# A hybrid decoder layer: the Mamba branch in a written-out TensorE order, with one z projection moved

## The chip, the cores and the metric

The kernel runs on one core of a Trainium2 chip. Its engines are TensorE (PE in the profile, with PEld for its weight loads), VectorE (DVE), ScalarE (ACT), GpSimd (POOL) and SyncE (SP, which here only issues DMAs). The metric is the device time of one execution in microseconds (us); several runs are summed up by their median.

## What is computed

One decoder layer on x (512 tokens of 1024 features, float32). A combined projection feeds an attention branch, a Mamba-2 branch and two gates; both branches are projected back, merged and projected, and then follow a layer norm, a SwiGLU feed-forward block and a second layer norm. The change lies in the Mamba branch, which has four groups of eight heads:

```python
def mamba2_branch(z, xbc, dt_raw, conv_w, conv_b, dt_bias, a_log, d_skip, norm_w):
    xbc = silu(causal_depthwise_conv(xbc, conv_w, conv_b))
    xs, bm, cm = split(xbc)
    dt = softplus(dt_raw + dt_bias)
    a = -exp(a_log)
    y = ssd_chunked(xs, dt, a, bm, cm) + d_skip[:, None] * xs
    u = (y * silu(z)).reshape(bsz, seq, SSM_GROUPS, -1)
    u = u * rsqrt(mean(square(u), -1) + RMS_EPS)
    return u * norm_w
# ssd_chunked, for each chunk of 128 tokens:
#   decay = exp(acum_l - acum_s) below the diagonal, acum = cumsum(dt * a)
#   y_diag = (C B^T * decay) (x dt);  state of the chunk = B^T (x dt decay_to_end)
#   h = h_prev * chunk_decay + state;  y_off = exp(acum) * C h_prev
```

## The kernel before

Every wide product is made of three matmuls (`mm3`, L144 to L147), since each operand is split into a high part and a low part (`split`, L102: ScalarE writes the high part, VectorE the rest). A **step** below is one such `mm3` with 512 columns. Weights come in chunks of 512 KB on SP's queue into four `raw` slots (`fetch_w`); three slots each hold the split halves. PSUM has four banks for wide accumulations (`gps`) and four for everything else (`cps`).

For each group g the Mamba branch does this:

- `group_bc` projects B and C (two blocks of 8 steps). `conv_evac` applies the convolution of four taps (ScalarE, three VectorE operations at L282) and a tanh, `silu_to` one more VectorE operation. Then B is transposed to token order (L306) and C·B of each chunk is formed and masked (L312, L313).
- `group_x` projects half of x (16 steps, two blocks), evacuates each in the same way and transposes it into `xtok` (L328, L329). It is called twice a group.
- `group_z` projects z (four banks, 32 steps) and writes tanh-gated values into the only `gz` slot (L337, L338).
- `group_y` runs over the four chunks: xdt on VectorE (L355); for each half of the heads a decay block loaded by SP from DRAM (`ac_d`, L361), five ScalarE operations on it (L364, L365), and a product with C·B on VectorE (L366); the y products (L370); dx on POOL (L373); the sum (L376); the product with the state of the chunks before (L379) and its two VectorE operations (L381, L382); xw on POOL (L385), the new state (L387) and its update (L392, L393).
- `group_u` multiplies y by the gate (L403), squares and sums it (ScalarE, L405), takes the power -1/2 on POOL (L407), scales (L408), transposes (L412) and splits.
- `group_proj` multiplies u by a quarter of the projection (32 steps) and adds the result to `sd` (ScalarE for group 0, VectorE at L424 otherwise).

Which instruction comes when: a scheduler at build time plays the program through with its own costs, and gives each engine the ready instruction of the best priority. Priorities follow the text of the program; inside `high_priority` they are raised. Inside `manual_schedule(engines=...)` the named engines keep the order of the text. On the chip each engine then executes its list strictly in that order. In the kernel before, the first z projection has TensorE, ScalarE and VectorE in text order; ScalarE stays so until `entry.close()`, which stands behind the softplus of dt and the exponential of a_log. The Mamba branch behind it (L588 to about L690) leaves TensorE to the scheduler, and the attention stage that follows has TensorE in text order again:

```python
    for g in range(NG):
        ys = group_y(g, st)
        if g == 0:
            st = group_bc(1)
            group_x(1, st, 0)
        else:
            group_proj(g - 1, u)
            gz = group_z(g)
        u = group_u(g, ys, gz)
```

Of the kernel before, what the change touches and what calls it, by code (L numbers as in the profile page):

```python
# [18 lines left out]
P = 128  # L19
# [23 lines left out]
def tile_hybrid_decoder_layer(  # L43
# [247 lines left out]
    def group_bc(g):  # L291
        st = {}
# [5 lines left out]
        for bi, nm in ((0, "bT"), (1, "cT")):  # L298
            v, th = conv_evac(16 + 4 * bi + g, gp[bi])
            st[nm] = slot(nm)  # L300
            silu_to(st[nm], v, th)
        bT, cT = st["bT"], st["cT"]
        btok = st["btok"] = slot("btok")
        ps = cps()
        for c in range(NT):
            nc.tensor.transpose(out=ps[:, c * P:(c + 1) * P], in_=bT[:, c * P:(c + 1) * P], identity=ident)  # L306
        nc.scalar.copy(out=btok, in_=ps)
        cbm = st["cbm"] = slot("cbm", (P, NT, P))
        ps = cps()
        for c in range(NT):  # L310
            cs = slice(c * P, (c + 1) * P)
            nc.tensor.matmul(out=ps[:, cs], lhsT=bT[:, cs], rhs=cT[:, cs], start=True, stop=True)  # L312
        nc.vector.tensor_tensor(out=cbm, in0=ps.rearrange("p (c l) -> p c l", c=NT),  # L313
                                in1=tri.rearrange("p (o l) -> p o l", o=1).broadcast_to([P, NT, P]), op=ALU.mult)
        st["xtok"] = big("xtok")
        return st

    def group_x(g, st, pair):
        xtok = st["xtok"]

        def evac(b, ps):
            j = 2 * pair + b
            v, th = conv_evac(4 * g + j, ps)
            xst = slot("xst")
            silu_to(xst, v, th)
            pt = cps()
            for c in range(NT):
                nc.tensor.transpose(out=pt[:, c * P:(c + 1) * P], in_=xst[:, c * P:(c + 1) * P], identity=ident)  # L328
            nc.scalar.copy(out=xtok[:, :, j * P:(j + 1) * P], in_=pt.rearrange("p (c f) -> p c f", c=NT))  # L329
        gemm_ws(w_in, C_X + g * 512 + pair * 256, KD, rhs_x, evac)  # L330
# [820 lines left out]
```

## Time and profile before

| | |
|---|---|
| median of 3 runs | 1131.83 us (1131.39 to 1133.82) |
| the profiled execution | 1133.8 us, span 1132.1 us |
| TensorE busy | 1104.3 us (98% of the span), 6086 matmuls |
| VectorE busy | 777.6 us (69%) |
| ScalarE busy | 526.7 us (47%) |
| GpSimd busy | 134.4 us (12%) |
| DMA | 134.20 MB, mean 119 GB/s |

The span is what the profile sees of one execution; the time of the run lies a little above it. Busy time of TensorE counts each matmul with a modelled end, and dense matmuls overlap, so the start times of neighbouring matmuls say more about lost time than the busy share does.

### The profile page before, as it was taken

The numbers are of one execution on the slowest core, as the hardware profiler recorded it, in microseconds if no ns is written. First come the engines' busy times: TensorE is split into PE (matmuls) and PEld (weight loads), VectorE is DVE, ScalarE is ACT, GpSimd is POOL, SyncE is SP. The second block draws the span as 40 slices with busy tenths as digits, with TensorE's granted clock in tenths as the row PEclk, the third lists the DMA queues.
The fourth block names the chain that finished last, engine by engine and source line by source line (L and its number), as shares of the span: only waits on it lengthen the run. The fifth ranks groups of instructions, "written<-read, shape, count | busy, mean of one in ns | idle before, by whom it ended". The sixth has DMA issues, their size and how long they took to land.

```text
span 1132.1 us, 15815 instructions
## 1 busy us (share of the span) xinstructions
PE 1104.3 (98%) x6086; PEld 942.8 (83%) x6086; DVE 777.6 (69%) x1223; ACT 526.7 (47%) x912; POOL 134.4 (12%) x165
## 2 busy tenths in 40 slices
PE   7999999999999999999999999999999999999996
PEld 5887778777787878888888888888999999988885
DVE  2679973885688473788778744556997777777326
ACT  2477764454442341567566544313654555453210
POOL 3003130020114000122110000011111111100001
PEclk9999999999999999999999999999999999999999
DMA  6353243243231333321222135381788787565212
GB/s 198 111 169 108 84 128 93 75 124 100 75 94 59 94 91 93 91 61 57 75 75 75 57 114 184 101 214 42 210 197 208 184 204 159 103 233 176 93 56 75
DMA packets 116059, 134.20 MB, mean 119 GB/s; under 512 B 5668, under 2 KB 94480, under 8 KB 115856
## 3 DMA queue, kind: packets, MB, share of 16 engines
q1 hardware_dynamic: 98896, 111.75, 32.3%
q0 software_dynamic: 14640, 14.10, 7.6%
q10 hardware_dynamic: 2448, 7.34, 1.9%
q8 instruction: 48, 0.79, 0.3%
q14 instruction: 27, 0.22, 0.1%
HBM read 128.78 MB, written 4.26 MB: 118 GB/s over the span
## 4 chain that ended last, share of the span: by engine, by line
PE 80%; DVE 9%; issue 4%; DMA 3%; POOL 2%; ACT 2%; POOLq 0%; DVEq 0%; ACTq 0%
PE gps L147 19%; PE gps L146 19%; PE gps L145 19%; PE cps L146 5%; PE cps L147 5%; PE cps L145 4%; PE cps L509 2%; DVE wlo L104 2%; PE cps L370 1%; PE cps L499 1%; ACT whi L103 1%; DMA rq<-in_w_ffn_up_dram 1%; PE cps L474 1%; PE cps L475 1%; PE cps L328 1%
## 5 line engine op out<-in xcount | busy, mean ns | idle before, releaser
L104 DVE TENSOR_TENSOR wlo<-raw,whi 128x1024 fp32r<-128x1024 f32 x127 | 156.2, 1230 | 176.4 <-ACT whi L103 175.1
L103 ACT CAST whi<-raw 128x1024 fp32r<-128x1024 f32 x127 | 133.5, 1051 | 244.3 <-PE gps L146 97.8
L145 PE MATMUL gps<-xh,whi 128*128 128x512 f32 x456 | 180.9, 397 | 0.0
L147 PE MATMUL gps<-xh,wlo 128*128 128x512 f32 x456 | 179.6, 394 | 0.0
L146 PE MATMUL gps<-xl,whi 128*128 128x512 f32 x456 | 179.3, 393 | 0.0
L103 ACT CAST wh<-rq 128x1024 fp32r<-128x1024 f32 (+1 forms) x84 | 82.1, 979 | 94.5 <-PE cps L146 42.7
L104 DVE TENSOR_TENSOR wl<-rq,wh 128x1024 fp32r<-128x1024 f32 (+1 forms) x84 | 94.8, 1132 | 29.5 <-ACT wh L103 29.3
L147 PEld LDWEIGHTS gps<-xh,wlo 128*128 128x128 f32 x456 | 86.1, 189 | 17.5
L145 PEld LDWEIGHTS gps<-xh,whi 128*128 128x128 f32 x456 | 86.0, 189 | 17.3 <-issue 0.2
L146 PEld LDWEIGHTS gps<-xl,whi 128*128 128x128 f32 x456 | 86.0, 189 | 17.3 <-issue 0.2
L145 PE MATMUL gps<-whi,xh 128*128 128x512 f32 x192 | 76.3, 398 | 1.9 <-ACT whi L103 1.6
L146 PE MATMUL gps<-wlo,xh 128*128 128x512 f32 x192 | 75.6, 394 | 1.2 <-DVE wlo L104 1.2
L147 PE MATMUL gps<-whi,xl 128*128 128x512 f32 x192 | 75.5, 393 | 0.0
L282 DVE SCALAR_TENSOR_TENSOR t_v<-gps,cw,t_v 128x511 f32<-128x511 f32 (+2 forms) x72 | 53.4, 744 | 3.8 <-ACT t_v L279 3.1
L146 PE MATMUL gps<-t_ul,whi 128*128 128x512 f32 x128 | 51.1, 399 | 0.0
L147 PE MATMUL gps<-t_uh,wlo 128*128 128x512 f32 x128 | 51.0, 399 | 0.0
L145 PE MATMUL gps<-t_uh,whi 128*128 128x512 f32 x128 | 50.5, 395 | 0.0
L481 ACT ACTIVATE t_y<-t_y,sm 128x128 f32<-128x128 f32 (+1 forms) x64 | 35.6, 558 | 21.1 <-DVE sm L479 21.0
L145 PEld LDWEIGHTS gps<-whi,xh 128*128 128x128 f32 x192 | 36.4, 190 | 10.5 <-ACT whi L103 2.3
L146 PEld LDWEIGHTS gps<-wlo,xh 128*128 128x128 f32 x192 | 36.4, 190 | 9.4 <-DVE wlo L104 2.0
L364 ACT ACTIVATE t_ab<-t_ab,acum 128x128 f32<-128x128 f32 x128 | 41.6, 391 | 4.7 <-DMA t_ab<-ac_d 2.7
L147 PEld LDWEIGHTS gps<-whi,xl 128*128 128x128 f32 x192 | 36.3, 189 | 8.5 <-DVE xl L104 1.1
(567 smaller groups left out, 2717.0 us busy)
## 6 DMA issues: line engine op xcount, KB each, us to landing
raw<-in_w_in_dram SPq DMA_DIRECT2D x80, 512.0 KB, 3.7
rq<-in_w_ffn_gate_dram SPq DMA_DIRECT2D x25, 512.0 KB, 5.9
rq<-in_w_ffn_up_dram SPq DMA_DIRECT2D x25, 512.0 KB, 6.3
raw<-in_w_ffn_down_dram SPq DMA_DIRECT2D x22, 512.0 KB, 3.8
t_ab<-ac_d SPq DMA_DIRECT2D x32, 256.0 KB, 3.2
raw<-in_w_proj_ssm_dram SPq DMA_DIRECT2D x16, 512.0 KB, 3.5
rq<-in_w_ffn_gate_dram POOLq DMA_DIRECT2D x10, 512.0 KB, 8.4
rq<-in_w_ffn_up_dram POOLq DMA_DIRECT2D x10, 512.0 KB, 6.2
```

The source lines that it names most:

```text
L103: nc.scalar.copy(out=hi, in_=src)
L104: nc.vector.tensor_tensor(out=lo, in0=src, in1=hi.bitcast(F32), op=ALU.subtract)
L145: nc.tensor.matmul(out=o, lhsT=l[0], rhs=r[0], start=start, stop=False, skip_group_check=skip)
L146: nc.tensor.matmul(out=o, lhsT=l[0], rhs=r[1], start=False, stop=False, skip_group_check=skip)
L147: nc.tensor.matmul(out=o, lhsT=l[1], rhs=r[0], start=False, stop=stop, skip_group_check=skip)
L282: nc.vector.scalar_tensor_tensor(out=v[:, sh:], in0=ps[:, 0:T - sh], scalar=cw[:, k, blk:blk + 1], in1=v[:, sh:], op0=ALU.mult, op1=ALU.add)
L328: nc.tensor.transpose(out=pt[:, c * P:(c + 1) * P], in_=xst[:, c * P:(c + 1) * P], identity=ident)
L364: nc.scalar.activation(out=m[:, r, :], in_=m[:, r, :], func=AF.Relu, scale=-1.0, bias=acum[:, c, h:h + 1])
L370: nc.tensor.matmul(out=py[:, r * 64:(r + 1) * 64], lhsT=ms[r // 4][:, r % 4, :], rhs=xdt[:, r * 64:(r + 1) * 64], start=True, stop=True)
L474: nc.tensor.matmul(out=ps[:, 0:n], lhsT=q1[:, qs], rhs=k1[:, 0:n], start=True, stop=False)
L481: nc.scalar.activation(out=pt[:, 0:n], in_=pt[:, 0:n], func=AF.Exp, scale=-1.0, bias=sm[:, 2:3], accum_out=sm[:, 0:1])
L509: nc.tensor.matmul(out=po[:, kb * P:], lhsT=vt[:, kb, hh, :], rhs=pT[kb][j], start=kb == 0 and j == 0, stop=kb == NT - 1 and j == 1)
```

## The change

The functions of the Mamba branch become generators that yield after every step. TensorE's order from the first B and C projection to the last Mamba projection is now the order of the text (`manual_schedule`), and the text deals out the steps: `run(steps, n)` takes n steps of the wide products, `pace(steps, ns, what)` alternates between them and the parts of `what` (the parameters, y or u), which it issues with raised priority. Small products that need an evacuation first (the transposes of B and of x, C·B) are put into `later` and issued 14 or 15 steps on. The evacuations of B, C and x get raised priority. In y, xw and dx are issued ahead of the y products, xw first, and the state's update ahead of the sums. In u, the norms of all four chunks come first and the transposes later, one chunk every three steps. The z projection of group 1 moves from behind the projection of group 0 to between the two halves of x of group 1; z of groups 2 and 3 stays where it was. `params` holds what stood behind the dt projection: softplus, cumulative sums and the transposes and DMA of the decay. Of its two exponentials, that of a_log stays in ScalarE's ordered part (now directly behind the copy of the dt projection), and that of the softplus leaves it.

```diff
-    def group_bc(g):
+
+    later = []
+
+    def run(steps, n=10 ** 6):
+        for _ in range(n):
+            if next(steps, 0) == 0:
+                return
+            for e in later:
+                e[0] -= 1
+            while later and later[0][0] <= 0:
+                later.pop(0)[1]()
+
+    def bc_steps(g, st):
         gp = [gps() for _ in range(2)]
+
+        def b_tok():
...
+            nc.scalar.copy(out=btok, in_=ps)
...
+        def c_b():
...
         for bi, c0 in ((0, C_B + g * P), (1, C_C + g * P)):
             hi, lo = load_w(w_in[:, c0:c0 + P], 8, P)
             for kt in range(KD):
                 mm3(gp[bi], (hi[kt], lo[kt]), rhs_x(kt), kt == 0, kt == KD - 1)
+                if kt == KD - 1:
+                    nm = ("bT", "cT")[bi]
+                    with tc.high_priority():
+                        v, th = conv_evac(16 + 4 * bi + g, gp[bi])
+                        st[nm] = slot(nm)
+                        silu_to(st[nm], v, th)
+                    later.append([14, (b_tok, c_b)[bi]])
+                yield 1
...
+    def x_steps(g, st, pair):
+        if pair == 0:
+            st["xtok"] = big("xtok")
         xtok = st["xtok"]
...
+            with tc.high_priority():
+                v, th = conv_evac(4 * g + j, ps)
+                xst = slot("xst")
+                silu_to(xst, v, th)
+
+            def to_tokens():
...
+                with tc.high_priority():
+                    nc.scalar.copy(out=xtok[:, :, j * P:(j + 1) * P], in_=pt.rearrange("p (c f) -> p c f", c=NT))
+            later.append([15, to_tokens])
+        yield from ws_steps(w_in, C_X + g * 512 + pair * 256, KD, rhs_x, evac)
...
+        if before is None:
+            return gz, xs_steps(w_in, C_Z + g * 512, lhs_x, evac)
...
-    def group_y(g, st):
+    def y_steps(g, st, ys):
...
+            if c < NT - 1:
+                xw = slot("xw")
+                nc.gpsimd.tensor_tensor(out=v8(xw), in0=v8(xc), in1=bc8(dtw, c), op=ALU.mult)
+            dx = slot("dx")
+            nc.gpsimd.tensor_tensor(out=v8(dx), in0=v8(xc),
+                                    in1=d_bc[:, h8].rearrange("p (h o) -> p h o", o=1).broadcast_to([P, 8, 64]), op=ALU.mult)
+            yield 1
             py = cps()
             for r in range(8):
                 nc.tensor.matmul(out=py[:, r * 64:(r + 1) * 64], lhsT=ms[r // 4][:, r % 4, :], rhs=xdt[:, r * 64:(r + 1) * 64],
                                  start=True, stop=True)
-            dx = slot("dx")
-            nc.gpsimd.tensor_tensor(out=v8(dx), in0=v8(xc),
-                                    in1=d_bc[:, h8].rearrange("p (h o) -> p h o", o=1).broadcast_to([P, 8, 64]), op=ALU.mult)
-            y = slot("y")
...
             if c > 0:
                 po = cps()
...
-                yo = slot("yo")
-                nc.vector.tensor_tensor(out=v8(yo), in0=v8(po), in1=bc8(ecum, c), op=ALU.mult)
-                nc.vector.tensor_tensor(out=y, in0=y, in1=yo, op=ALU.add)
             if c < NT - 1:
-                xw = slot("xw")
-                nc.gpsimd.tensor_tensor(out=v8(xw), in0=v8(xc), in1=bc8(dtw, c), op=ALU.mult)
...
+            y = slot("y")
+            nc.vector.tensor_tensor(out=y, in0=py, in1=dx, op=ALU.add)
+            if c > 0:
+                yo = slot("yo")
+                nc.vector.tensor_tensor(out=v8(yo), in0=v8(po), in1=bc8(ecum, c), op=ALU.mult)
+                nc.vector.tensor_tensor(out=y, in0=y, in1=yo, op=ALU.add)
             ys.append(y)
-        return ys
-
-    def group_u(g, ys, gz):
+            yield 1
...
+    def u_steps(g, ys, gz):
...
+        yield 1
...
             pu = cps()
...
             split(uh[:, :, cs], ul[:, :, cs], pu.rearrange("p (j t) -> p j t", j=4))
-        return uh, ul
-
-    def group_proj(g, u):
-        uh, ul = u
+            yield 1
...
     ea = carve(SH)
     nc.scalar.activation(out=ea, in_=a_bc, func=AF.Exp)
     entry.close()
-    da = carve(NT, SH)
...
+    def params():
+
+        ps = cps()
+        for tt in range(NT):
+            nc.tensor.transpose(out=ps[:, tt * 48:(tt + 1) * 48], in_=fdT[0:48, tt * P:(tt + 1) * P], identity=ident[0:48, 0:48])
...
+        yield 1
+        daf = da.rearrange("p t h -> p (t h)")
+        ps = cps()
+        nc.tensor.matmul(out=ps[:, 0:128], lhsT=tri, rhs=daf, start=True, stop=True)
+        nc.tensor.matmul(out=ps[:, 128:256], lhsT=ones, rhs=daf, start=True, stop=True)
...
+        yield 1
+        acT = carve(T)
+        ps = cps()
+        for tt in range(NT):
+            nc.tensor.transpose(out=ps[0:32, tt * P:(tt + 1) * P], in_=acum[:, tt, :], identity=ident)
+        nc.scalar.copy(out=acT[0:32], in_=ps[0:32])
+        nc.sync.dma_start(out=ac_d.rearrange("c h l -> h c l"), in_=acT[0:32].rearrange("h (c l) -> h c l", c=NT))
...
+        yield 1
...
-    st = group_bc(0)
-    for pair in range(2):
-        group_x(0, st, pair)
-    nw_bc = slot("nw", (P, 2048))
-    nc.sync.dma_start(out=nw_bc, in_=ssm_norm_w.partition_broadcast(P))
+    sts = [{} for _ in range(NG)]
     qk = {}
-    u = None
-    for g in range(NG):
-        ys = group_y(g, st)
-        if g == 0:
-            st = group_bc(1)
-            group_x(1, st, 0)
-        else:
-            group_proj(g - 1, u)
-            gz = group_z(g)
-        u = group_u(g, ys, gz)
-        if g == 0:
-            group_x(1, st, 1)
-        elif g < NG - 1:
-            st = group_bc(g + 1)
-            for pair in range(2):
-                group_x(g + 1, st, pair)
-    for isq in (True, False):
-        for _ in att_qk(0, isq, qk):
-            pass
-    group_proj(NG - 1, u)
+    u = [None]
+
+    def pace(steps, ns, what):
+
+        for n in ns:
+            run(steps, n)
+            with tc.high_priority():
+                next(what)
+
+    def bcx(g):
+        return chain(bc_steps(g, sts[g]), x_steps(g, sts[g], 0), x_steps(g, sts[g], 1))
+
+    def z_steps(g):
+        gz[0], steps = group_z(g)
+        yield from steps
+
+    gz = [gz]
+    with tc.manual_schedule(engines={mybir.EngineType.PE}):
+        after = bcx(0)
+        pace(after, (3, 20, 5), params())
+        nw_bc = slot("nw", (P, 2048))
+        nc.sync.dma_start(out=nw_bc, in_=ssm_norm_w.partition_broadcast(P))
+        run(after)
+        for g in range(NG):
+            after = bcx(g + 1) if g < NG - 1 else chain(att_qk(0, True, qk), att_qk(0, False, qk))
+            ys = []
+            if g == 0:
+                after = chain(bc_steps(1, sts[1]), x_steps(1, sts[1], 0), z_steps(1), x_steps(1, sts[1], 1))
+                run(after, 16)
+                pace(after, (0, 2, 0, 5, 0, 5, 0, 4), y_steps(g, sts[g], ys))
+                pace(after, (0, 9, 3, 3, 3), u_steps(g, ys, gz[0]))
+            elif g == 1:
+                steps = chain(proj_steps(g - 1, *u[0]), after)
+                run(steps, 16)
+                pace(steps, (0, 4, 0, 6, 0, 6, 0, 6), y_steps(g, sts[g], ys))
+                pace(steps, (0, 9, 3, 3, 3), u_steps(g, ys, gz[0]))
+                run(steps)
+            else:
+                steps = chain(proj_steps(g - 1, *u[0]), z_steps(g))
+                run(steps, 16)
+                pace(steps, (0, 4, 0, 6, 0, 6, 0, 6), y_steps(g, sts[g], ys))
+                run(steps)
+                pace(after, (0, 7, 3, 3, 3), u_steps(g, ys, gz[0]))
+            run(after)
+        run(proj_steps(NG - 1, *u[0]))
+    assert not later
```

## Rows read from the trace of the kernel before

**Rows 1.** The page: TensorE's busy time, and the chain that ended last.

```profile
PE 1104.3 (98%) x6086; PEld 942.8 (83%) x6086; DVE 777.6 (69%) x1223; ACT 526.7 (47%) x912; POOL 134.4 (12%) x165
...
PE 80%; DVE 9%; issue 4%; DMA 3%; POOL 2%; ACT 2%; POOLq 0%; DVEq 0%; ACTq 0%
```

**Rows 2.** Waits of TensorE, 44 to 460 us: total, times, longest.

```profile
PE cps L412 <- DVE t_y L408: 3.7, 6, 0.7
PE cps L370 <- DVE t_ab L366: 1.8, 3, 0.7
PE cps L387 <- POOL t_xw L385: 1.2, 4, 0.3
PE cps L312 <- DVE ss L406: 0.6, 1, 0.6
```

**Rows 3.** Timeline of TensorE around group 1's u transposes (start, duration, us).

```profile
196.98 0.39 PE L145 MATMUL gps<-xh,whi 128*128 128x512 f32 x1
197.21 0.39 PE L146 MATMUL gps<-xl,whi 128*128 128x512 f32 x1
198.11 0.63 PE L412 MATMUL cps<-ident,t_y 128*128 128x128 f32 x4 [0.52 <-DVE t_y L408]
...
201.79 0.39 PE L146 MATMUL gps<-xl,whi 128*128 128x512 f32 x1
202.26 0.66 PE L412 MATMUL cps<-ident,t_y 128*128 128x128 f32 x4
```

**Rows 4.** Timeline of the other engines there, u's norm chain.

```profile
195.46 0.63 ACT L405 ACTIVATE t_sq<-t_y 128x512 f32<-128x512 f32 x1
...
196.08 0.69 DVE L403 SCALAR_TENSOR_TENSOR t_y<-t_y,t_gz 128x512 f32<-128x512 f32 x1
...
196.19 0.99 POOL L407 TENSOR_TENSOR ss<-ss,neghalf 128x1 f32<-128x1 f32 x1 [36.18 <-DVE ss L406]
...
197.21 0.75 DVE L408 SCALAR_TENSOR_TENSOR t_y<-t_y,ss,t_nw 128x512 f32<-128x512 f32 x1 [0.44 <-POOL ss L407]
```

**Rows 5.** Timeline of TensorE at group 0's first y products.

```profile
94.02 0.39 PE L145 MATMUL gps<-xh,whi 128*128 128x512 f32 x1
94.33 0.63 PE L328 MATMUL cps<-ident,t_xst 128*128 128x128 f32 x4
94.72 0.47 PE L146 MATMUL gps<-xl,whi 128*128 128x512 f32 x1
95.03 0.39 PE L147 MATMUL gps<-xh,wlo 128*128 128x512 f32 x1
...
96.46 1.97 PE L370 MATMUL cps<-t_xdt,t_ab 128*128 128x64 f32 x16
98.72 1.12 PE L387 MATMUL cps<-t_xw,t_btok 128*128 128x512 f32 x2 [0.29 <-POOL t_xw L385]
```

**Rows 6.** xdt, xw and dx by tile: least, median, longest ns; first, last start.

```profile
L355 DVE TENSOR_TENSOR t_xdt<-t_xtok,dt x16: 679/693/1534, 95.6 to 349.0; 128x512 f32<-128x512 f32 x16
...
L385 POOL TENSOR_TENSOR t_xw<-t_xtok,dtw x12: 1040/1486/1509, 97.2 to 349.4; 128x512 f32<-128x512 f32 x12
...
L373 POOL TENSOR_TENSOR t_dx<-t_xtok,d_bc x16: 1043/1422/1552, 95.7 to 352.7; 128x512 f32<-128x512 f32 x16
```

**Rows 7.** DMA issues of the page: KB each, us to landing.

```profile
raw<-in_w_in_dram SPq DMA_DIRECT2D x80, 512.0 KB, 3.7
```

**Rows 8.** VectorE's groups, 44 to 460 us: busy us, mean ns, idle before.

```profile
L104 DVE TENSOR_TENSOR wlo<-raw,whi 128x1024 fp32r<-128x1024 f32 x60 | 74.2, 1237 | 75.8 <-ACT whi L103 75.7
...
L366 DVE TENSOR_TENSOR t_ab<-t_ab,t_cbm 128x512 f32<-128x512 f32 x32 | 23.0, 736 | 0.6 <-ACT t_ab L365 0.5
...
L355 DVE TENSOR_TENSOR t_xdt<-t_xtok,dt 128x512 f32<-128x512 f32 x16 | 14.7, 940 | 0.8 <-ACT t_xtok L329 0.8
```

**Rows 9.** Stage of group 0's y: length, PE, PEld, DVE, ACT, POOL busy, PEclk.

```profile
96.40:137.10 40.70, 39.84 (x213) 31.77 (x213) 37.42 (x56) 29.83 (x68) 12.28 (x11) 1.00 0.34 105
```

**Rows 10.** The slice with the cumulative sums, columns as in rows 9.

```profile
56.60:84.90 28.30, 28.15 (x143) 23.23 (x142) 20.07 (x32) 20.52 (x46) 0.00 (x0) 0.94 0.58 169
```

More of the change, by code (lines that the diff above doesn't have):

```diff
@@ L289, in silu_to @@
         nc.vector.scalar_tensor_tensor(out=o, in0=th, scalar=1.0, in1=v, op0=ALU.add, op1=ALU.mult)
-    def group_bc(g):
-        st = {}
-        gp = [gps() for _ in range(2)]
+    later = []
[8 more added lines that the diff above has]
+    def bc_steps(g, st):
+        gp = [gps() for _ in range(2)]
+        def b_tok():
+            btok = st["btok"] = slot("btok")
+            ps = cps()
+            for c in range(NT):
+                nc.tensor.transpose(out=ps[:, c * P:(c + 1) * P], in_=st["bT"][:, c * P:(c + 1) * P], identity=ident)
+            nc.scalar.copy(out=btok, in_=ps)
+        def c_b():
+            cbm = st["cbm"] = slot("cbm", (P, NT, P))
+            ps = cps()
+            for c in range(NT):
+                cs = slice(c * P, (c + 1) * P)
+                nc.tensor.matmul(out=ps[:, cs], lhsT=st["bT"][:, cs], rhs=st["cT"][:, cs], start=True, stop=True)
+            nc.vector.tensor_tensor(out=cbm, in0=ps.rearrange("p (c l) -> p c l", c=NT),
+                                    in1=tri.rearrange("p (o l) -> p o l", o=1).broadcast_to([P, NT, P]), op=ALU.mult)
         for bi, c0 in ((0, C_B + g * P), (1, C_C + g * P)):
@@ L409, in group_u @@
                                            op0=ALU.mult, op1=ALU.mult)
+        yield 1
+        for c in range(NT):
+            cs = slice(c * P, (c + 1) * P)
+            y = ys[c]
             pu = cps()
@@ L413, in group_u, with proj_steps @@
             split(uh[:, :, cs], ul[:, :, cs], pu.rearrange("p (j t) -> p j t", j=4))
-        return uh, ul
-    def group_proj(g, u):
-        uh, ul = u
+            yield 1
+    def proj_steps(g, uh, ul):
         for pair in range(4):
@@ L623, in tile_hybrid_decoder_layer @@
     entry.close()
-    da = carve(NT, SH)
-    nc.vector.scalar_tensor_tensor(out=da, in0=dt, scalar=-1.0, in1=ea.rearrange("p (o c) -> p o c", o=1).broadcast_to([P, NT, SH]),
-                                   op0=ALU.mult, op1=ALU.mult)
-    daf = da.rearrange("p t h -> p (t h)")
-    ps = cps()
-    nc.tensor.matmul(out=ps[:, 0:128], lhsT=tri, rhs=daf, start=True, stop=True)
-    nc.tensor.matmul(out=ps[:, 128:256], lhsT=ones, rhs=daf, start=True, stop=True)
-    for tt in range(NT):
-        o = ps[:, 256 + tt * AH:256 + (tt + 1) * AH]
-        for u in range(tt):
-            nc.tensor.matmul(out=o, lhsT=ones, rhs=lf[:, u, :], start=u == 0, stop=False)
-        nc.tensor.matmul(out=o, lhsT=tri, rhs=lf[:, tt, :], start=tt == 0, stop=True)
+    dt = cst.tile([P, NT, SH], F32, name="dt")
```

133 lines of the change are left out of this document (53 added, 80 removed).

## The prediction, made before the changed kernel was run

> **What bounds the kernel now.** I read the page first, then TensorE's waits over the Mamba stretch (44 to 460 us), then the timeline around each wait, then busy time by stage, then VectorE's groups of that stretch. The page says that TensorE is busy 98% of the span and holds 80% of the chain that ended last, VectorE 9% [rows 1]. So only two things can move the end: TensorE stops that go away, and TensorE stops that appear. The change leaves every matmul in place, and its fetches bring the same bytes; all of it lies between about 44 us (the first B and C products) and 460 us.
>
> How much stop is there? The view of waits lists 14: six for the normed y that the u transposes read, three for the decay block, four for POOL's xw, one before the C·B products; 3.7 + 1.8 + 1.2 + 0.6 = 7.3 us [rows 2]. That is too little by a fixed amount each: the page models a wide matmul as 0.39 us long, while dense ones start 0.23 us apart (196.98 and 197.21) [rows 3], so each listed wait hides about 0.16 us more. 14 x 0.16 = 2.2, together 9.5 us. The timeline shows one kind that the list leaves out: the second u transposes of groups 1 to 3 start 0.47 us after the matmul ahead of them (201.79 to 202.26) where 0.23 is normal, 3 x 0.24 = 0.7 us [rows 3]. So 10.2 us of stops, 0.9% of the span, is the most that a better order can give back, clock aside. The reader should see how small this is: the old order was already good.
>
> **What each part does, step by step.**
>
> *u transposes of groups 1 to 3.* In the old order the products of z are followed closely by u's four clusters of transposes, and TensorE stands for them: 197.21 to 198.11 is 0.90 us where 0.23 is normal [rows 3], and there are two such stops and one short one in each of the three groups. What they wait for is a chain of VectorE, ScalarE, VectorE, POOL, VectorE, of which VectorE itself waits 0.44 us for POOL [rows 4]. In the new order the norms of all four chunks are issued first and the transposes come 9, 12, 15, 18 steps later (7, 10, 13, 16 for groups 2 and 3). A step is three matmuls, 0.68 us, so the first cluster has 7 x 0.68 = 4.8 us behind z's last step, and its own z part was evacuated up to 6 steps (4.1 us) earlier. That is more than the about 4 us that the norm chain of one chunk takes (0.69 for y times gate, 0.63 for the squares, 0.99 for the power on POOL, 0.75 for the scaling, two short instructions and the hops: an estimate from [rows 4]). For group 1 z lies a whole stage earlier, so its u waits for y alone. I take all of this as gone: 3.7 + 6 x 0.16 + 0.7 = 5.4 us.
>
> *y products.* The decay blocks cost 1.8 + 3 x 0.16 = 2.3 us, POOL's xw 1.2 + 4 x 0.16 = 1.8 us [rows 2]. xw is now issued ahead of dx and both ahead of the y products; at 98.72 TensorE waits 0.29 us for xw because dx (median 1.42 us) ran first [rows 5, 6]. Chunks lie 4 to 6 steps apart, 2.7 to 4.1 us, instead of back to back. Both kinds go, 4.1 us.
>
> *C·B products.* They are put off 14 steps behind C's last product, 9 us; the wait of 0.6 + 0.16 = 0.8 us goes [rows 2]. Sum removed: 5.4 + 4.1 + 0.8 = 10.3, the same 10.2 within rounding.
>
> *The parameter chain* (softplus, cumulative sums, decay write to DRAM) keeps its place: 3 steps, then 20, then 5, where the old order had nearly the same distances. ScalarE's exponential of a_log no longer stands behind the softplus exponential in the ordered part. The decay write and the loads of the decay blocks go out on SP's queue about as early as before, and norm weights behind them; the first y products come only at 96.46 [rows 5], some 30 us behind the cumulative sums, which hides this. If that cover were gone, the block loads would cost their landing once, an estimated 3.7 us, that of a weight fetch [rows 7]. I count 0.
>
> *z of group 1* moves ahead by two stages, with its four fetches of 512 KB, past the second half of x, the projection of group 0 and their fetches on SP's queue. The four raw slots limit how far ahead any of them go, before and after, so the cost is 0; if a fetch were late, its landing time (3.7 us) once [rows 7]. Its evacuation writes the only gz slot, so it queues behind u of group 0, whose norms are issued first. What is gained is room for VectorE: 32 steps with little VectorE work now lie beside u of group 0.
>
> **What is added.** TensorE can no longer pass over an instruction that isn't ready: everything behind it waits. The unknown is whether VectorE keeps up where y lies between steps. A middle chunk of y costs VectorE 0.94 (xdt) + 2 x 0.74 (decay times C·B) + about five more, taken at the same 0.74, 6.1 us; the first one 3.2, the last 4.6, a group 20 us [rows 8]. Group 0, 16 steps: TensorE needs 16 x 0.68 = 10.9 plus the y products, about 2.0 a chunk for the 16 narrow ones and 1.1 for each of six wide pairs, less overlap, together 14, so 25 us [rows 5]. VectorE needs 20 for y, 2 x 3.0 for the convolutions of C and of x's third block (four operations at 0.74), 0.7 for the mask, 2 x 1.24 for splits: 29 us, of which 4.4 (six decay blocks, which have six slots) can be done ahead [rows 8]. That is 25 against 25: full. The stage of the old order with the same work ran VectorE 37.42 of 40.70 us, and TensorE lost under 1 us in it (39.84 busy) [rows 9]. Bounds for group 0: nothing, or 0.66 us (the longest listed wait is 0.7) for each of four chunks and once for z's fourth bank, 3.3 us; I take 1.5, nearer to the old stage. Groups 1 to 3 have 22 steps, 15 + 14 = 29 us, against 20 for y, three splits (3.7) and, in two of the groups, about five additions of the projection (3.7), so 24 to 28 us of VectorE with 4.4 done ahead: slack. Bounds 0 and 4 x 0.66 each; I take 0.3 each, 0.9 in all, since the old order with denser chunks lost 0.7 to 0.8 per group.
>
> Leaving the stream of wide products has a price too: 94.02 to 95.03 holds two wide matmuls and four transposes, 0.31 + 0.39 + 0.31 us where 0.23 + 0.39 + 0.23 would do, so 0.16 us a change [rows 5]. The old order runs up to three chunks of y in one cluster and joins other clusters; I count about 3 entries more per group in the new, 12 x 0.12 to 0.16: I take 1.4 us. Bounds 0 (they merge) and 2.5.
>
> *The shared port.* xdt usually takes 0.69 us, but up to 1.53, and POOL's xw 1.04 to 1.51 [rows 6]: the long ones lie beside POOL's work on the same xtok. Now xw and xdt are released together, so this may hit more often. By the rows VectorE loses 16 x (0.94 - 0.69) = 4.0 us to it now; if every xdt were hit it would be 16 x 0.84 = 13.4 us. The Trainium skill ("SBUF — State Buffer", section "SBUF: two separate sides") says that a GpSimd instruction and a VectorE instruction with two SBUF inputs exclude each other for the whole instruction, whoever starts first; the trace agrees in direction, its longest xdt being 0.84 us over the median. By that rule the larger sum would be the usual one, and it speaks against the change. For TensorE I keep the terms above, since four steps or more (2.7 us) lie between the token transposes and the products that need xdt.
>
> *Clock.* One slice around 62 us shows a granted share of 0.94 of 28.3 us [rows 10], that is about 3.4 us at the lower of the two levels (1.2 instead of 2.4 GHz), right behind the narrow cumulative-sum products. At most 1.7 us is lost there. The same products stand in the same order, so I count no change.
>
> **Sum.** 1133.8 (the profiled execution; its span is 1132.1) - 10.3 + 1.5 + 0.9 + 1.4 = 1127.3 us. The profiled execution is 2.0 us above the median of the three runs (1131.83), so on their footing 1125.3 us, 0.6% less. With all costs at nothing it would be 1121.5, with the clock's loss gone too about 1120; with all at their upper bounds (3.3 + 7.9 + 2.5) it is 1135.2.
>
> **Rivals.**
> - *The stops move.* VectorE's backlog in the y stretches, group 0 above all, makes new stops as large as the old ones: 1131.8, within 2.3 us. For it: group 0's balance of 25 against 25. Against it: the same balance cost little in the old order [rows 9].
> - *Slower: xdt and decay blocks behind POOL.* With xw released beside xdt, VectorE loses 0.84 us in each chunk and TensorE, held to its order, stands for it: 16 x 0.84 = 13.4 of new stops, with 1.4 for entries against 10.3: 1131.8 + 4.5 = 1136.3. It decides from (10.3 - 1.4) / 16 = 0.56 us a chunk. The page of the Trainium skill named above gives this rule. For it: the longest xdt, and that TensorE already waits three times for a decay block [rows 2, 6]. Against it: the distance of 2.7 to 4.1 us.
> - *Nothing new appears and the clock stays up*: 1120 to 1121.5.
> - That the change does nothing is not likely: the order of TensorE is set by hand afterwards.
>
> **Chances.** Forecast (1122 to 1129.5) 0.61, no new stops 0.09, stops move 0.17, slower 0.13. This kernel's runs lie 0.2% apart, so 0.2% (2.3 us) is about what a measurement can tell from no change. Faster by over that 0.70, within it 0.17, slower 0.13. The range reaches from the floor, 1119.5, into the slower case, 1134.0, leaving out about 0.12.
>
> **What will show it.** Right: no TensorE wait on y for the u transposes, none on xw; z of group 1 at about 120 to 145 us between x halves; the end of the last Mamba projection about 6 us earlier, and all behind it shifted by the same. Wrong: waits of the y products on the decay blocks or xdt of over 0.5 us in most chunks; a stop before z's fourth bank; a stop at the cumulative sums of some us with a longer low clock; or a late weight split, seen as wide matmuls that wait for the low part.

## The result, and the profile after

The changed kernel takes 1123.71 us in the median (7 executions, 1123.18 to 1129.63) where the kernel before takes 1132.81 beside it on the same chip (7, 1131.39 to 1134.11): a ratio of 0.9933, with a 95% interval of 0.992 to 0.9946. It is faster by 0.7%. The forecast was 1125.3, and the range of 1119.5 to 1134.0 holds the result. The profiled execution has 1123.71 us and a span of 1121.9 us, 10.2 us less than before. The end of the last Mamba projection lies 10.2 us earlier too (its last product starts at 428.2 instead of 438.4 us), so all that was won lies in the Mamba stretch and nothing is lost behind it.

First the page: TensorE's busy time, and the chain that ended last, which answer to [rows 1].

```profile
PE 1098.1 (98%) x6086; PEld 944.6 (84%) x6086; DVE 776.8 (69%) x1223; ACT 526.9 (47%) x912; POOL 128.9 (11%) x165
...
PE 85%; DVE 7%; issue 3%; DMA 2%; ACT 1%; POOL 0%; POOLq 0%; DVEq 0%; ACTq 0%
```

The same 6086 matmuls; TensorE's share of the chain rose from 80 to 85%, and POOL's fell from 2% to nothing. Then TensorE's waits from 44 to 460 us, which answer to [rows 2] (total, times, longest):

```profile
PE cps L446 <- DVE t_y L438: 3.6, 2, 2.9
PE cps L671 <- DVE t_y L666: 0.2, 1, 0.2
```

Of the 14 waits of before none is left in groups 1 to 3, at the y products or at C·B. What is left is new and stands in one place, the u transposes of group 0 (L446 was L412 before). Here is TensorE's timeline there (start, duration; the bracket is the idle time before and its releaser):

```profile
132.47 0.40 PE L147 MATMUL gps<-whi,xl 128*128 128x512 f32 x1
133.57 0.63 PE L446 MATMUL cps<-ident,t_y 128*128 128x128 f32 x4 [0.70 <-DVE t_y L438]
...
135.88 0.39 PE L147 MATMUL gps<-whi,xl 128*128 128x512 f32 x1
139.16 0.66 PE L446 MATMUL cps<-ident,t_y 128*128 128x128 f32 x4 [2.89 <-DVE t_y L438]
```

From start to start the two stops are 1.10 and 3.28 us where 0.23 is normal, so 0.87 + 3.05 = 3.9 us are lost. VectorE's list in the same stretch says why:

```profile
130.28 1.89 DVE L392 TENSOR_TENSOR t_ab<-t_ab,t_cbm 128x512 f32<-128x512 f32 x3
132.08 0.68 DVE L104 TENSOR_TENSOR t_ul<-cps,t_uh 128x512 fp32r<-128x512 f32 x1
132.68 0.74 DVE L438 SCALAR_TENSOR_TENSOR t_y<-t_y,ss,t_nw 128x512 f32<-128x512 f32 x1
133.34 1.89 DVE L392 TENSOR_TENSOR t_ab<-t_ab,t_cbm 128x512 f32<-128x512 f32 x3
135.14 0.68 DVE L104 TENSOR_TENSOR t_ul<-cps,t_uh 128x512 fp32r<-128x512 f32 x1
135.75 0.68 DVE L433 SCALAR_TENSOR_TENSOR t_y<-t_y,t_gz 128x512 f32<-128x512 f32 x1
...
138.35 0.75 DVE L438 SCALAR_TENSOR_TENSOR t_y<-t_y,ss,t_nw 128x512 f32<-128x512 f32 x1 [0.73 <-POOL ss L437]
```

Six decay products of group 1 (L392, 3.8 us), which TensorE needs only over 40 us later, stand ahead of the gating (L433) of group 0's last chunk and around the scaling (L438) of the chunk before. The transposes at 139.16 stand behind them. Three windows (length, then busy time and count of PE, PEld, DVE, ACT and POOL, PEclk, DMA share, GB/s) give the balance:

```profile
97.20:120.20 23.00, 23.00 (x131) 18.49 (x130) 22.89 (x33) 16.92 (x41) 8.29 (x8) 1.00 0.39 116
120.20:149.10 28.90, 25.31 (x122) 20.35 (x121) 20.25 (x32) 14.82 (x31) 1.10 (x2) 1.00 0.30 89
56.60:84.90 28.30, 28.07 (x150) 23.45 (x149) 20.58 (x35) 19.30 (x43) 0.00 (x0) 1.00 0.56 170
```

While group 0's y runs, VectorE is full (22.89 of 23.00 us) and TensorE doesn't stop once. In z's stretch behind it VectorE has 8.6 us to spare, and there TensorE stops. The third line answers to [rows 10]: the clock's fall behind the cumulative sums, 0.94 there, is absent in this execution.

At last an ordinary entry into narrow work, TensorE's timeline in the projection of group 1, against [rows 5]:

```profile
238.72 0.39 PE L147 MATMUL gps<-t_uh,wlo 128*128 128x512 f32 x1
238.95 0.60 PE L350 MATMUL cps<-ident,t_xst 128*128 128x128 f32 x4
239.31 0.48 PE L145 MATMUL gps<-t_uh,whi 128*128 128x512 f32 x1
239.63 0.39 PE L146 MATMUL gps<-t_ul,whi 128*128 128x512 f32 x1
```

Wide matmul, four transposes, wide, wide: 0.23 + 0.36 + 0.32 = 0.91 us from the first start to the last, where the same row of work took 1.01 before. Ahead of the transposes nothing is lost now, 0.23 us where it was 0.31. So that part of what the prediction took for the price of leaving the wide stream reads as a short wait that no bracket shows. The 0.32 behind them is still there.

### The profile page after: what moved, and what is told of

Same layout as the page of the kernel before. It is cut to its first block, busy times and chain, and to the rows that moved or that the text cites. A ratio compares the mean times of both kernels' runs of the same rounds, so it can differ in the third digit from the quotient of the medians.

```text
span 1121.9 us, 15816 instructions
## 1 busy us (share of the span) xinstructions
PE 1098.1 (98%) x6086; PEld 944.6 (84%) x6086; DVE 776.8 (69%) x1223; ACT 526.9 (47%) x912; POOL 128.9 (11%) x165
## 4 chain that ended last, share of the span: by engine, by line
PE 85%; DVE 7%; issue 3%; DMA 2%; ACT 1%; POOL 0%; POOLq 0%; DVEq 0%; ACTq 0%
PE gps L147 20%; PE gps L146 20%; PE gps L145 20%; PE cps L146 5%; PE cps L147 5%; PE cps L145 5%; PE cps L403 2%; PE cps L542 2%; PE cps L532 1%; DVE wlo L104 1%; DMA rq<-in_w_ffn_up_dram 1%; PE cps L410 1%; PE cps L407 1%; PE cps L507 1%; PE cps L508 1%
## 5 line engine op out<-in xcount | busy, mean ns | idle before, releaser
L145 PE MATMUL gps<-xh,whi 128*128 128x512 f32 x456 | 184.2, 404 | 0.0
L145 PE MATMUL gps<-whi,xh 128*128 128x512 f32 x192 | 78.9, 411 | 1.9 <-ACT whi L103 1.6
L282 DVE SCALAR_TENSOR_TENSOR t_v<-gps,cw,t_v 128x511 f32<-128x511 f32 (+2 forms) x72 | 53.6, 744 | 5.8 <-ACT t_v L279 5.2
L145 PE MATMUL gps<-t_uh,whi 128*128 128x512 f32 x128 | 52.9, 413 | 0.0
```

The source lines that it names most:

```text
L145: nc.tensor.matmul(out=o, lhsT=l[0], rhs=r[0], start=start, stop=False, skip_group_check=skip)
L282: nc.vector.scalar_tensor_tensor(out=v[:, sh:], in0=ps[:, 0:T - sh], scalar=cw[:, k, blk:blk + 1], in1=v[:, sh:], op0=ALU.mult, op1=ALU.add)
```

## The experiments

All times are medians of the executions on one chip beside the kernel before: 1132.59 for e1 to e4, 1132.15 for e6 to e9, 1132.18 for e5 and e10 to e12. "Clock" is the mean granted clock of an execution. The new stop is called the u stop.

**e1, the changed kernel again.**

> The changed kernel once more, unaltered, to see how its time goes with the granted clock: its seven runs so far fall into three sets, 1123.2 to 1123.7 us at a granted clock of 0.998, 1126.1 at 0.995, and 1128.8 to 1129.6 at 0.992. My theory: the order took away 10.2 us of TensorE stops and added one of 3.9 us at u of group 0, and the clock falls (or not) in an execution of its own accord, worth up to 5.5 us. It expects again about 1123.5 with a clock of 0.998 in most executions and 1126 to 1130 wherever the clock is 0.995 or lower, and the profile to show a TensorE stop of about 3 us before the last u transposes of group 0. Rival: the spread has nothing to do with the clock; then times over 1126 come at 0.998 too.

1124.42 (6 executions, 1123.45 to 1128.32), ratio 0.9932 [0.9919, 0.9945]; the same two u stops, 0.60 and 3.05 us. Five executions have a clock of .996 or .997 and 1123.45 to 1124.87 us, one has .992 and 1128.32. With those of the result, 3 of 13 executions are at .992 and lie about 5 us above the others: 1123.18 to 1123.71 at .998, 1128.83 and 1129.63 at .992.

**e2, the last two u clusters of group 0 later.**

```diff
-                pace(after, (0, 9, 3, 3, 3), u_steps(g, ys, gz[0]))
+                pace(after, (0, 9, 3, 9, 6), u_steps(g, ys, gz[0]))
```

> The u transposes of group 0 come later among z's steps (9, 12, 21 and 27 steps behind y instead of 9, 12, 15 and 18). Theory: the two stops of 0.87 and 3.05 us there are a local lateness of the norms; with 6 and 9 steps (4.1 and 6.1 us) more in front they go, and the time falls by 3.5 to 3.9 us, to about 1119.8 at the same clock; nothing else moves. If the longer stop is also what lets the clock fall, the executions at 0.992 go as well. Rival: VectorE is in debt and passes the lateness on; then z's last evacuations or the next convolutions are late instead, a new stop of 2 to 4 us appears behind, and the time stays at 1123.7 within 1 us.

1119.71 (1119.67 to 1119.80), 0.9886 [0.9872, 0.9901]. The u stop is gone and nothing takes its place; the longest wait left is 0.3 us. All four executions are at .998. Against the executions of the changed kernel at .998 (1123.2 to 1123.7) the u stop costs 4 us, and with it goes the scatter.

**e8, the paced steps without their raised priority.**

```diff
-            with tc.high_priority():
-                next(what)
+            next(what)
```

> The changed kernel, with its own places of the u transposes, but y, u and the parameters dealt out without the raised priority. In the changed kernel VectorE does six decay products of group 1 (3.8 us) ahead of the last two norms of u of group 0. Theory: that order is what makes the two stops of 3.9 us there; without the raised priority the norms come first in VectorE's list, the stops shrink under 1 us, and the time is 1119.7 to 1121, with no execution at a clock under 0.995. Rival: VectorE is simply in debt from y of group 0 (it is busy 22.9 of 23.0 us there); then a stop of 2 to 4 us stays, or moves to y, and the time is 1122 to 1125.

1119.46 (1119.15 to 1120.10), 0.9887 [0.9874, 0.9901]. TensorE's order is written out and doesn't change, only the lists of the other engines. VectorE's list at u of group 0:

```profile
126.35 0.74 DVE L438 SCALAR_TENSOR_TENSOR t_y<-t_y,ss,t_nw 128x512 f32<-128x512 f32 x1
...
128.95 0.75 DVE L438 SCALAR_TENSOR_TENSOR t_y<-t_y,ss,t_nw 128x512 f32<-128x512 f32 x1
...
130.49 0.75 DVE L438 SCALAR_TENSOR_TENSOR t_y<-t_y,ss,t_nw 128x512 f32<-128x512 f32 x1
...
131.76 2.49 DVE L392 TENSOR_TENSOR t_ab<-t_ab,t_cbm 128x512 f32<-128x512 f32 x4
```

The norms now come ahead of the decay products, the last scaling at 130.49 instead of 138.35, and TensorE is busy 28.90 of 28.90 us in the window where it was 25.31. That shows the cause of the u stop: not VectorE's load but its list, in which the raise had put the next group's decay products ahead of this group's norms. In e2 the stop is covered by more steps instead. e2 and e8 are the best versions found, 1.1% under the kernel before and 0.4% under the changed one.

**e3, z of group 1 back behind the projection of group 0**, the rest as changed.

```diff
-                after = chain(bc_steps(1, sts[1]), x_steps(1, sts[1], 0), z_steps(1), x_steps(1, sts[1], 1))
...
-            elif g == 1:
...
```

> The one move undone: z of group 1 stands behind the projection of group 0 again, as for groups 2 and 3, and the rest of the new order stays. Theory: the order is what counts; z between the halves of x gives VectorE room beside u of group 0, without it the x evacuations (about 3 us of VectorE per block) fall into that stretch, and the stops at u of group 0 grow from 3.9 to 5 to 8 us: 1125 to 1128. Rival A: the move is what brought the gain; then the time goes back to about 1130 or more, with stops at u of group 1. Rival B: the move does harm, since u of group 0 would not stop without it; then about 1120.

1130.72 (11 executions, 1130.01 to 1131.81), 0.9985 [0.9977, 0.9994]. Both theories had something wrong: the size is larger than that of mine, and the place isn't the rival's. TensorE's waits from 44 to 460 us, and the window behind the longest:

```profile
PE cps L446 <- DVE t_y L438: 5.4, 2, 4.8
PE gps L145 <- ACT t_uh L103: 0.7, 1, 0.7
PE gps L146 <- DVE t_ul L104: 0.4, 1, 0.4
```

```profile
137.10:147.30 10.20, 7.61 (x20) 5.24 (x21) 7.33 (x12) 4.14 (x7) 0.55 (x1) 0.50 0.17 52
```

The u stop of group 0 is longer, and the projection of group 0 waits for u's last split. From 0.9 us before the end of the long stop the clock is at half, 1.2 instead of 2.4 GHz, for 10.2 us, and all 11 executions have a clock of .992 or .993.

**e11, e8 with z of group 1 back**: the same edit, without the raise that disturbs e3.

> Built on the kernel without raised priority for y, u and the parameters (1119.5 us). z of group 1 goes back behind the projection of group 0. Theory: with the raised priority this cost 7 us (stops of 5.6 and 3.4 us at u of group 0 and a low clock after them); part of that was the same wrong order in VectorE's list, part is VectorE's real load with bc, x, x, y and u in one stage. So a part remains: stops of 2 to 5 us, 1121.5 to 1125. Rival A: the list was all of it; then within 0.7 us of 1119.5 and the move is worth nothing by itself. Rival B: the load is all of it; then 1127 or more.

1128.01 (1126.15 to 1128.22), 0.996 [0.9947, 0.9972], so 8.5 us above e8.

```profile
PE gps L145 <- ACT t_uh L103: 2.2, 1, 2.2
PE gps L146 <- DVE t_ul L104: 1.9, 1, 1.9
```

```profile
135.01 0.60 PE L446 MATMUL cps<-ident,t_y 128*128 128x128 f32 x4
137.77 0.50 PE L145 MATMUL gps<-t_uh,whi 128*128 128x512 f32 x1 [2.16 <-ACT t_uh L103]
140.22 0.80 PE L146 MATMUL gps<-t_ul,whi 128*128 128x512 f32 x1 [1.95 <-DVE t_ul L104]
```

The norms are early now, and still TensorE stops, a step later: the projection of group 0 stands for the split of u's last chunk, because no other work is left to cover it. That can be counted in the code. With z away the stage has 16 + 16 + 16 = 48 steps (B and C, two halves of x), and the paces use 16, 16 for y and 18 for u, 50 in all: the last transposes come two steps early, and none is left behind them. With z it has 80, and 30 are left. The two stops lose 2.4 + 2.1 = 4.5 us from start to start. Of 6.8 us at half clock 5.9 lie behind them and cost some 2.7 (a wide matmul starts every 0.43 us there instead of 0.23), and this profile has 3.4 us at half clock behind the cumulative sums, which e8's lacks, 1.2 to 1.7 us: together they cover the 8.5. The time is the one that rival B gave, but that VectorE's load is all of it isn't shown: in ScalarE's and VectorE's lists the split also stands behind x's evacuation, which has raised priority, and z back with more steps behind the transposes wasn't tried.

**e9, the move alone**: the kernel before with only z of group 1 between the halves of x.

```diff
-            gz = group_z(g)
+            if g > 1:
+                gz = group_z(g)
...
+            gz = group_z(1)
```

> The kernel before with nothing but the move: z of group 1 between the halves of x of group 1, TensorE's order still left to the scheduler. Theory: the move matters only beside the written order, where u of group 0 would otherwise run into the x evacuations; alone it changes little, since the stops at u of groups 2 and 3 and at y stay: 1130 to 1133. It can take at most the stops of group 1's u, 1.8 us. Rival: the move is the larger part of the gain; then 1127 or less.

1131.82 (11 executions, 1130.06 to 1133.84), 0.9993 [0.9984, 1.0002]: no difference. Its waits against [rows 2]:

```profile
PE cps L412 <- DVE t_y L408: 2.5, 4, 0.7
PE cps L370 <- DVE t_ab L366: 1.3, 2, 0.7
PE cps L387 <- POOL t_xw L385: 1.1, 4, 0.3
...
PE cps L370 <- DVE t_xdt L355: 0.7, 1, 0.7
```

Two of the waits at u go and one at xdt comes. The move is worth 0.3 us, within the noise, where the scheduler chooses TensorE's order, and 6 to 8.5 us beside the written one (e3 against e1, e11 against e8): the paces need the room that it makes.

**e4, the order of TensorE left to the scheduler**, with the new text.

```diff
-    with tc.manual_schedule(engines={mybir.EngineType.PE}):
+    with ExitStack():
```

> The new text with its steps, delays, priorities and the moved z, but TensorE's order in the Mamba branch left to the scheduler at build time. Theory: the gain comes from the distance that the written order puts between a producer and the products that need it; the scheduler issues a product as soon as it reckons its input ready, so short stops come back at y, u and C*B, some 5 to 10 us in all: 1128 to 1133. Rival: the new text with its priorities is enough (for instance xw ahead of dx, raised evacuations), and the time stays within 1 us of 1123.7 or, without the stop at u of group 0, falls to 1120.

1128.76 (1126.89 to 1130.13), 0.9965 [0.9953, 0.9977]. The new text brings 3.8 us, the written order the other 4.3 (against e1), or 9 once the u stop is gone (against e2). The chunks of y come together again, and the sum that frees a PSUM bank for the next y products is late:

```profile
PE cps L403 <- DVE t_y L419: 3.0, 2, 2.2
PE cps L446 <- DVE t_y L438: 1.4, 2, 0.7
PE cps L407 <- DVE t_hn L416: 1.1, 1, 1.1
PE cps L403 <- DVE t_ab L392: 0.5, 1, 0.5
```

**e6, dense chunks of y in groups 1 to 3** (on e2).

```diff
-                pace(steps, (0, 4, 0, 6, 0, 6, 0, 6), y_steps(g, sts[g], ys))
+                pace(steps, (0, 4, 0, 1, 0, 1, 0, 16), y_steps(g, sts[g], ys))
```

> Built on the kernel with the later u of group 0 (1119.7 us at a steady clock). In groups 1 to 3 the y chunks stand 4, 1, 1 and 16 steps apart instead of 4, 6, 6 and 6, which is about the density that the old order had. Theory: the distance is what took the y stops away; with one step (0.7 us) between the second, third and fourth chunk the state's update on VectorE, xw on POOL and the sums are late again, 0.7 to 1.5 us per group as in the old order, so 2 to 4.5 us more: 1122 to 1124. Rival: the y stops went because xw is issued ahead of dx and the state's update ahead of the sums; then the time stays within 0.5 us of 1119.7.

1121.46 (1120.26 to 1121.99), 0.9903 [0.9889, 0.9916], with no wait at y. The one execution at .998 has 1120.26, 0.5 above e2; the others have a clock of .996 or .997. My theory, that the distance of 4 to 6 steps is what removed the stops at y, falls: chunks almost back to back wait for nothing.

**e10, e6 with the old text inside a chunk**: dx behind the y products, y's sums ahead of the update of the state, xw last.

```diff
-                xw = slot("xw")
...
-            dx = slot("dx")
...
             py = cps()
...
+            dx = slot("dx")
...
+            y = slot("y")
...
                 po = cps()
...
+                yo = slot("yo")
...
+                xw = slot("xw")
...
                 hprev = hn
-            y = slot("y")
...
-                yo = slot("yo")
```

> Built on the run with the y chunks 4, 1, 1 and 16 steps apart (1120.3 us at a clock of 0.998). Inside a chunk the text is that of the old kernel again: dx behind the y products, the sums ahead of the state's update, xw behind both. Theory: distance and order inside the chunk stand in for each other, and only with both taken back do the y stops of the old kernel (0.7 to 1.5 us a group) return: 2 to 4 us more, 1122 to 1124.5, waits on xw and on decay blocks or state in the profile. Rival: neither matters and TensorE's fixed place of the chunks behind the token transposes alone suffices; then it stays within 0.5 us of 1120.3.

1126.32 (1125.47 to 1128.91), 0.9953 [0.994, 0.9967], 4.9 above e6, more than expected. The stop is at another place than I thought, not at xw but at the state (L406 here; 4.2, 2 times, longest 3.4 us). VectorE's list ahead of the longest, which ends at 185.98:

```profile
181.90 0.68 DVE L408 TENSOR_TENSOR t_yo<-cps,ecum 128x512 f32<-128x512 f32 x1
...
183.35 0.68 DVE L409 TENSOR_TENSOR t_y<-t_y,t_yo 128x512 f32<-128x512 f32 x1
183.96 0.68 DVE L403 TENSOR_TENSOR t_y<-cps,t_dx 128x512 f32<-128x512 f32 x1
184.56 0.68 DVE L431 SCALAR_TENSOR_TENSOR t_y<-t_y,t_gz 128x512 f32<-128x512 f32 x1
185.15 0.68 DVE L420 TENSOR_TENSOR t_hn<-t_hn,cps 128x512 f32<-128x512 f32 x1
```

The state hn, for which the next matmul waits, stands behind four operations of sums and gating that this matmul doesn't need. So with the new order inside a chunk the distance isn't needed (e6), and without both y loses about 5 us, part of it at half clock behind the stop. But both stops lie where u's gating and norms already stand among y's sums: the longer one in group 1 and one of 0.8 us in group 0, which keeps its distances of 5 steps. Groups 2 and 3, whose z and so whose gating come later, are as dense and in the same old order, and have no stop at all. There neither the distance nor the new order inside a chunk was needed.

**e7, u of groups 2 and 3 early** (on e2).

```diff
-                pace(after, (0, 7, 3, 3, 3), u_steps(g, ys, gz[0]))
+                pace(after, (0, 3, 5, 1, 1), u_steps(g, ys, gz[0]))
```

> Built on the same kernel. For groups 2 and 3 the u transposes come 3, 8, 9 and 10 steps behind z's last step instead of 7, 10, 13 and 16. Theory: 5.4 us of the gain was the distance between the norm chain (about 4 to 5 us a chunk) and its transposes; with 3 steps (2.0 us) less cover for the first and 4 us less for the last chunk, one or two stops of 0.5 to 2 us come back in each of the two groups, so 2 to 5 us: 1121.7 to 1124.7. Rival: the norms, now issued for all four chunks at once, are early anyway; then the time stays within 0.5 us of 1119.7.

1131.25 (10 executions, 1130.29 to 1138.68), 0.9997 [0.9982, 1.0012]: the whole gain is gone, 11.5 us, far more than expected. (The execution of 1138.68 has a clock of .942; no profile shows why.)

```profile
PE cps L446 <- DVE t_y L438: 7.5, 2, 4.7
```

```profile
299.30:302.70 3.40, 3.40 (x11) 2.83 (x12) 1.06 (x2) 0.59 (x1) 1.57 (x3) 0.51 0.02 2
398.30:401.70 3.40, 3.40 (x10) 2.62 (x9) 1.18 (x3) 1.10 (x2) 0.00 (x0) 0.50 0.02 5
```

The two stops, 4.7 and 2.8 us, end at 299.2 and 397.6, and behind each come 3.4 us at half clock, up to 1.7 us lost a piece: 7.5 + 3.4 = 10.9 of the 11.5. The stops are larger than the old ones at u (3.7 us in three groups), so it is not only these that come back. VectorE's list ahead of the first says why:

```profile
291.94 0.68 DVE L433 SCALAR_TENSOR_TENSOR t_y<-t_y,t_gz 128x512 f32<-128x512 f32 x1
...
294.28 0.74 DVE L282 SCALAR_TENSOR_TENSOR t_v<-gps,cw,t_v 128x511 f32<-128x511 f32 x1
...
296.79 0.74 DVE L282 SCALAR_TENSOR_TENSOR t_v<-gps,cw,t_v 128x509 f32<-128x509 f32 x1
...
298.32 0.75 DVE L438 SCALAR_TENSOR_TENSOR t_y<-t_y,ss,t_nw 128x512 f32<-128x512 f32 x1 [0.73 <-POOL ss L437]
```

The last norm of group 2 stands behind the next group's convolution (L282), and from its gating to its scaled end it takes 7 us. In the changed kernel it stands there too: in group 2 the last scaling ends at 300.79, and its transposes start at 301.43. So the distance of the prediction was needed, and had 0.6 us to spare.

**e5, dx ahead of xw on POOL** (on e2).

```diff
-            if c < NT - 1:
-                xw = slot("xw")
...
             dx = slot("dx")
...
+            if c < NT - 1:
+                xw = slot("xw")
```

> Built on the kernel with the later u of group 0 (1119.7 us). dx goes ahead of xw on POOL again, everything else stays. Theory, after the run with dense y chunks lost only 0.5 us at the same clock: the distance hides either order, so up to 0.5 us more at the first chunk of each group (dx takes 1.0 to 1.5 us, four to six steps lie in front): 1119.7 to 1120.2. Rival: xw ahead of dx is what took the xw waits away; then 1.2 to 1.8 us more, 1121 to 1121.5, with TensorE waits on xw in the profile.

1120.58 (1119.84 to 1122.29), 0.9901 [0.9887, 0.9914]; 1119.84 and 1119.88 at .998, 0.15 above e2, and no wait for xw. The order of the two on POOL is worth nothing here.

**e12, the cumulative sums in two parts** (on e8): those of the attention's gate four steps after those of the decay.

```diff
-        pace(after, (3, 20, 5), params())
+        pace(after, (3, 20, 4, 3), params())
```

> Built on the kernel without raised priority (1119.2 to 1119.7 us at 0.998, 1120.1 at 0.997). The narrow products of the cumulative sums, some 2.7 us in one piece, are parted: those of dt first, those of the forget gates four steps later. Theory: in the kernels before and after, the low clock of 3.4 us around 62 to 67 us comes right behind this piece in some executions and costs 1.1 to 1.7 us; in two pieces it does not come, so every execution is at 0.998 and 1119.0 to 1119.7. Rival: the low clock there has nothing to do with that piece; then about a third of the executions still show 0.996 to 0.997 with 1120 to 1121.

1120.36 (1120.06 to 1121.07), 0.9899 [0.9884, 0.9914], 0.9 above e8, with two executions at .998 and two at .997. Inconclusive: no gain, and the parting doesn't keep the clock's fall away in all executions.

## Why the prediction was right, and where its terms were off

The direction and the mechanism hold: the stops that the profile of before listed went away, and the last Mamba projection ends earlier by as much as the span is shorter. The gain is 9.1 us in the medians where 6.5 were forecast. By its own steps:

- *Stops removed, 10.3 us: right, but not the most that there was.* The stops at u of groups 1 to 3, at the decay blocks, xw and C·B are all gone. The prediction called 10.2 us the most that a better order can give back, clock aside. e8's span is 14.3 us shorter than that of before, of which the clock is at most 1.7, so 12.6 were there. For u the distance from the norms is needed (e7), but the norm chain of a last chunk takes 6.5 us in group 2 and not about 4, since the next group's convolution stands in it. For y the prediction named the distance and the early xw, and neither is what did it: dense chunks don't wait (e6), and dx ahead of xw costs nothing (e5). In groups 0 and 1 the state's update ahead of the sums is needed, with u's work in the same list (e10). In groups 2 and 3 what is left, as far as the runs go, is the written place of the chunks and their raised priority, which no run parts.
- *New stops at y, 1.5 and 0.9 us: mis-sized, measured 0.* VectorE is as full as worked out (25 of 25, measured 22.89 of 23.00), and yet no product of y waits.
- *Leaving the wide stream, 1.4 us: mis-sized, at most 0.4.* The same cluster takes 0.91 us instead of 1.01, so of the 0.16 a change 0.10 was a short wait of the old order. And the new order has 7 entries more into narrow work (58 against 51 in the two traces), not 12.
- *u of group 0: missed, the step that failed.* The sum held nothing for it; 3.9 us measured. The prediction saw the danger of group 0's backlog but looked for it at y, and counted room for VectorE beside u. The room was there (20.25 of 28.90 us busy) and the stop came even so, through the order of VectorE's list (e8).
- *z of group 1, 0 us: wrong as a price of its own.* Alone it is worth 0.3 us (e9), but beside the written order 6 to 8.5 (e3, e11). The prediction saw in it only room for VectorE. Without the move the paces use up the stage, 50 of 48 steps, and nothing covers the last split.
- *Clock, no change: off by up to 1.7 us in the profiled execution.* The piece of 3.4 us at half clock behind the cumulative sums is absent there, but e1's profile has it at 63.7 to 67.1 us. It comes in some executions of both kernels.

The account of the two profiled executions: -10.3 removed, +3.9 u stop, -1.7 clock is -8.1, and the spans differ by -10.2. Most of the missing 2.1 us are short waits at the old entries that no bracket shows: added up over the 0.23 us of a dense start, and without those that the 10.3 holds, that lie at half clock or that stand directly behind other narrow work, they come to 1.8 us before and 0.4 after. The last 0.7 us are not traced. Against the forecast of 1127.3 for that execution, the terms that came out at nearly nothing (1.5 + 0.9 + 1.4 = 3.8) and the missed stop (3.9) happen to cancel, which is luck, and the 3.6 us below it are the clock and mostly these short waits.

The rivals: *the stops move* was right in kind at one place, with 3.9 us and not 10. *Slower, through xdt beside POOL* didn't come. TensorE waits for no xdt, and its mean went from 0.94 to 0.87 us with a median of 0.69, so VectorE loses 16 x 0.18 = 2.9 us to the long ones instead of 4.0. The Trainium skill ("SBUF — State Buffer", section "SBUF: two separate sides") lets one engine block the other for a whole instruction. The trace agrees where the two run beside each other, but not in each chunk as the prediction had it: they do so at the first chunk of groups 0 to 2, and once more in group 0 (1.08 us). In group 1, VectorE's rows and then POOL's:

```profile
171.35 2.14 DVE L381 TENSOR_TENSOR t_xdt<-t_xtok,dt 128x512 f32<-128x512 f32 x2 [3.35 <-ACT t_xtok L352]
176.56 0.69 DVE L381 TENSOR_TENSOR t_xdt<-t_xtok,dt 128x512 f32<-128x512 f32 x1 [1.09 <-PE cps L403]
...
171.39 1.55 POOL L396 TENSOR_TENSOR t_xw<-t_xtok,dtw 128x512 f32<-128x512 f32 x1 [33.07 <-ACT t_xtok L352]
177.52 1.04 POOL L396 TENSOR_TENSOR t_xw<-t_xtok,dtw 128x512 f32<-128x512 f32 x1 [3.13 <-PE cps L410]
```

Two xdt take 2.14 us beside the first xw, as in groups 0 and 2, where two alone would take 1.29 (group 3, whose xw starts later). From the second chunk on xw has only one slot and waits for the state's product (L410), so it mostly starts when xdt is done. *Nothing new and the clock up*, 1120 to 1121.5, is what e2 and e8 reach after one more edit, even a little under it.

## What to carry to other kernels

Where an order is written out by hand, count for each stage the steps that it has against those that its paces use: 48 against 50, with none left to cover the last split, cost 8.5 us here, and an edit that makes room is worth nothing until the order needs it. A busy share doesn't show whether an engine will be late: VectorE kept up when it was 100% busy and was late at 70%, so read its list in order, and ask of each instruction ahead of the awaited one who needs it and when. Raising the priority of everything that is paced put work of the next group ahead of that of this one; leaving it away (e8) gave some 4 us.

## What was not expected of the hardware

- A short stop of TensorE in dense work can cost more than its length. In stops with an idle part of 1.9 to 4.8 us, or up to 0.8 us behind them, the granted clock went from 1.00 to 0.50 for 3.4 us (e7, twice), 6.8 us (e4, e10, e11) or 10.2 us (e3). In e4 the stretch behind the stop of 2.25 us, 110.0 to 116.8, is at 0.51 with TensorE busy in all of it. The changed kernel's stop of 2.9 us had no such piece in its profiled execution, and yet 3 of its 13 executions have a clock of .992 instead of .995 to .998 and are some 5 us longer than most. That the fall follows the u stop in those three is argued: the five kernels without that stop and without another in its place (e2, e5, e6, e8, e12) have no execution of 20 under .995, but the three have no profile of their own.
- The narrow cumulative-sum products are followed in 7 of the 14 profiles by 3.4 us at half clock, with no listed stop there or one of 0.2 us, which profiles without the fall have too: the changed kernel has none in one profile and it in the other (e1). It costs 1.2 to 1.7 us, which no edit here controlled (e12).
